# mLSTM stage of a hybrid trunk: element-wise work moved from GpSimd to VectorE, PSUM reads of h moved to ScalarE, state products moved first

## The chip, the cores and the metric

The kernel runs on one core of one Trainium2 chip. The metric is the device time of one execution in microseconds (us); less is better. The engines are named as the profile names them: PE (TensorE, matmul and transpose), PEld (TensorE's weight loads, which overlap its matmuls), DVE (VectorE), ACT (ScalarE), POOL (GpSimd) and SP (SyncE, which issues most of the transfers here).

## The reference

Two layers on a sequence of 2048 tokens with 1024 channels, in float32: first a layer with a matrix memory (mLSTM), then one with a gated linear recurrence (RG-LRU), then a final norm. The change lies in the heads of the first layer. There, for each of 4 heads:

```python
q = einsum('bshd,hde->bhse', xch, w_q) * (M_DK ** -0.5)   # xch: silu of a causal convolution of xm
k = einsum('bshd,hde->bhse', xch, w_k)
v = einsum('bshd,hde->bhse', xmh, w_v)
...
def step(carry, inp):                                     # one chunk of tokens
    C, n, m = carry
    ...
    Sm = einsum('bhtk,bhsk->bhts', qb, kb) * W
    num = decay * einsum('bhtk,bhkv->bhtv', qb, C) + einsum('bhts,bhsv->bhtv', Sm, vb)
    den = decay * einsum('bhtk,bhk->bht', qb, n) + sum(Sm)
    hb = num / max(abs(den), exp(-m_t))
    C_new = d_last * C + einsum('bhs,bhsk,bhsv->bhkv', w_last, kb, vb)
...
hh = o * h_tilde
hn = (hh - mean(hh)) * rsqrt(var(hh) + EPS) * norm_w
y = (hn + skip * xc) * silu(z)
return y @ w_out
```

A head has keys of 256 and values of 512 elements.

## The kernel before

A product of float32 operands is made as three products of a high and a low part: `split_into` rounds the source to the high part (ACT or DVE, L735 to L737) and subtracts to get the low part (DVE or POOL, L738); `mm3` (L362 to L364) issues high by high, low by high, high by low.

Three stages stand one behind another: one ahead that makes the convolved input, the gates and silu(z) and leaves them in DRAM; `phase_a2`, the stage of the heads, from about 1010 to 1724 us of the span; and from there on the output projection and the second layer. `phase_a2` goes over 4 heads, each in 8 blocks of 256 tokens, each block in 2 chunks of 128. It is software pipelined. For block i it issues, in this order:

- `loads` of block i+1: the transfers (all on SP), the splits of `xc` and `xm` into `xch`, `xcl`, `xmh`, `xml`, and a causal mask on `qb` by POOL (`affine_select`, L828). With the first block of a head come the head's four weight loads and their splits (`qwl`, `kwl` and two halves of `vwl`);
- `recur` of chunk 0 of block i: products of the masked scores with v into a PSUM tile `n`, the state products `kv` for m = 0 and 1 (one PSUM tile, so the second waits until the first was read by the DVE update of `C`), the products of q with the state's parts `Ch`, `Cl`; then DVE's denominator (`da`), `hh` and its statistics;
- `finish` of block i-1: ACT normalises `hh` (L971) with the scale and shift in `frs`, PE transposes it into PSUM (`pt`), DVE makes `y` from `pt`, the norm weight and `skx` (skip times xc), POOL multiplies by silu(z) and stores `d_y`;
- the q and k projections of block i+1 (`skx` is made by ACT ahead of them), `recur` of chunk 1 of block i (at its end come the aggregate of the statistics, `mv`, L957, and `frs`), the scores of block i+1 and its v projections (`vh`, `vl`).

The scheduler puts these into one queue for each engine, and each engine works its queue in order. The pools bound how far a block runs ahead: two buffers for `skx`, `qb`, `sz` and `y`, one for the parts of `xc` and `xm`, one PSUM tile each for `n` and `kv`.

Of the kernel before, what the change touches and what calls it, by code (L numbers as in the profile page):

```python
# [10 lines left out]
AF = mybir.ActivationFunctionType  # L11
ALU = mybir.AluOpType
# [12 lines left out]
KV = DV // P  # L25
# [263 lines left out]
class Trunk:  # L289
# [459 lines left out]
    def phase_a2(self, wq, wk, wv, D):  # L749
        tc, nc = self.tc, self.nc  # L750
        BL = 256
        NB = T // BL
        with ExitStack() as ctx:
# [21 lines left out]
            def head_weights(h):  # L775
                w = {}
                for nm, src in (("q", wq[h]), ("k", wk[h]), ("v0", wv[h, :, :, 0:256]), ("v1", wv[h, :, :, 256:512])):
                    raw = wp.tile([P, KV, 256], F32, tag="wraw", name="wraw", bufs=2)
                    nc.sync.dma_start(raw, src)
                    if nm[0] == "v":  # L780
                        j = int(nm[1])
                        if j == 0:
                            w["v"] = (wp.tile([P, KV, 512], F32R, tag="vwh", name="vwh"),
                                      wp.tile([P, KV, 512], F32R, tag="vwl", name="vwl"))
                        hi, lo = (t[:, :, j * 256:(j + 1) * 256] for t in w["v"])
                    else:
                        w[nm] = (wp.tile([P, KV, 256], F32R, tag=nm + "wh", name=nm + "wh"),
                                 wp.tile([P, KV, 256], F32R, tag=nm + "wl", name=nm + "wl"))
                        hi, lo = w[nm]
                    a = self.split_into(hi, lo, raw, "a", "v" if h == 0 and nm in ("k", "v1") else "p")  # L790
                    if h == 0 and nm in "qk":
                        self.order(a, self.tail[-4:])
                W[h] = w

            def project(h, b):
# [7 lines left out]
                def loads():  # L803
                    if h not in W:
                        head_weights(h)
                    xm = lp.tile([P, KV, BL], F32, tag="xm", name="xm")
                    xc = lp.tile([P, KV, BL], F32, tag="xc", name="xc")
                    nc.sync.dma_start(xc, D["xc"][hs, :, bs].rearrange("k p t -> p k t"))
                    nc.sync.dma_start(xm, D["xm"][hs, :, bs].rearrange("k p t -> p k t"))
                    S["qb"] = qb = lp.tile([P, 2, P], F32, tag="qb", name="qb")  # L810
                    S["db"] = db = lp.tile([P, BL], F32, tag="db", name="db")
                    nc.sync.dma_start(qb, D["q"][r0:r0 + 2].rearrange("c t -> (c t)").partition_broadcast(P)
                                      .rearrange("p (c t) -> p c t", c=2))
                    nc.sync.dma_start(db, D["dec"][r0:r0 + 2].rearrange("c t -> (c t)").partition_broadcast(P))
                    S["sz"] = sz = lp.tile([P, KV, BL], F32, tag="sz", name="sz")
                    S["o"] = o = lp.tile([P, 2, DV], F32, tag="o", name="o")
                    nc.sync.dma_start(sz, D["sz"][hs, :, bs].rearrange("k p t -> p k t"))
                    nc.sync.dma_start(o, D["o"][b * 2:b * 2 + 2, :, h * DV:(h + 1) * DV].rearrange("c p n -> p c n"))
                    for nm, x in (("xc", xc), ("xm", xm)):
                        hi = xp.tile([P, KV, BL], F32R, tag=nm + "h", name=nm + "h")  # L820
                        lo = xp.tile([P, KV, BL], F32R, tag=nm + "l", name=nm + "l")
                        fi = (h, b, nm) == (0, 0, "xc")
                        a = self.split_into(hi, lo, x, "v" if fi else "a", "v" if nm == "xc" else "p")
                        if fi:
                            self.order(a, self.tail[-4:])
                        S[nm] = (hi, lo)
                    S["xcf"] = xc
                    nc.gpsimd.affine_select(qb, qb, pattern=[[0, 2], [1, P]], compare_op=ALU.is_ge, fill=3.0e38,  # L828
                                            base=0, channel_multiplier=-1)
                    wgt = dp.tile([P, 2, P], F32, tag="wgt", name="wgt")  # L830
                    for c in range(2):
                        nc.scalar.activation(wgt[:, c], qb[:, c], AF.Exp, bias=self.gT[:, r0 + c:r0 + c + 1],
                                             scale=-1.0)
                    S["wgt"] = wgt
# [70 lines left out]
            def recur(h, b, c, S):  # L905
# [4 lines left out]
                sh, sl = (t[:, c] for t in S["sm"])  # L910
                pn = p1.tile([P, 2, 512], F32, tag="n", name="n")
                outs = tuple(pn[:, a, 0:258] for a in range(2))
                for a in range(2):
                    self.mm3(outs[a], sh, sl, vh[i][:, VA[a]], vl[i][:, VA[a]], True, ch == 0)

                def update(m):

                    kh, kl = (t[:, c] for t in S["kw"])
                    ms = slice(m * P, (m + 1) * P)
                    ps = p1.tile([P, 2, 512], F32, tag="kv", name="kv")  # L920
                    for a in range(2):
                        self.mm3(ps[:, a, 0:258], kh[:, ms], kl[:, ms], vh[i][:, VA[a]], vl[i][:, VA[a]], True, True)
                    Cm = sp.tile([P, 516], F32, tag=f"C{m}", name=f"C{m}") if ch == 0 else C[m][0]
                    C2, p2 = Cm.rearrange("p (a b) -> p a b", a=2), ps[:, :, 0:258]
                    if ch == 0:
                        nc.vector.tensor_copy(C2, p2)
                    else:
                        nc.vector.scalar_tensor_tensor(C2, C2, self.dl[:, r:r + 1], p2, op0=ALU.mult, op1=ALU.add)
                    Ch = dp.tile([P, 516], F32R, tag=f"Ch{m}", name=f"Ch{m}")
                    Cl = dp.tile([P, 516], F32R, tag=f"Cl{m}", name=f"Cl{m}")  # L930
                    self.split_into(Ch, Cl, Cm, "a", "v")
                    return Cm, (Ch, Cl)

                for m in range(2):
                    old = C.get(m) if ch > 0 else None
                    if ch < 15:
                        C[m] = update(m)
                    if ch > 0:
                        Hc, Lc = old[1]
                        qh, ql = (t[:, m, cs] for t in S["qd"])  # L940
                        for a in range(2):
                            self.mm3(outs[a], qh, ql, Hc[:, VA[a]], Lc[:, VA[a]], False, m == 1)
# [16 lines left out]
                if c == 1:  # L959
                    mv = S["mv"]  # L960
                    S["rs"] = rs = dp.tile([P, 2, 2], F32, tag="frs", name="frs")
                    nc.gpsimd.tensor_scalar(rs[:, 0], mv[:, 1], EPS, 1.0, op0=ALU.add, op1=ALU.mult)
                    nc.gpsimd.tensor_tensor(rs[:, 0], rs[:, 0], mh, op=ALU.pow)
                    nc.vector.scalar_tensor_tensor(rs[:, 1], mv[:, 0], -1.0, rs[:, 0], op0=ALU.mult, op1=ALU.mult)

            def finish(h, b, S):
                rs = S["rs"]
                y = lp.tile([P, KV, BL], F32, tag="y", name="y")
                for c in range(2):
                    hn = S["hh"][c]  # L970
                    nc.scalar.activation(hn, hn, AF.Identity, bias=rs[:, 1, c:c + 1], scale=rs[:, 0, c:c + 1])  # L971
                for j in range(2):
                    pt = pr.tile([P, 2, 2, P], F32, tag="r", name="pt")
                    for k in range(2):
                        for c in range(2):
                            ks = slice((j * 2 + k) * P, (j * 2 + k + 1) * P)
                            nc.tensor.transpose(pt[:, k, c], S["hh"][c][:, ks], self.ident)
                    for k in range(2):
                        kk = j * 2 + k
                        nc.vector.scalar_tensor_tensor(y[:, kk], pt[:, k].rearrange("p c t -> p (c t)"),  # L980
                                                       self.v("nw", h * KV + kk), S["skx"][:, kk],
                                                       op0=ALU.mult, op1=ALU.add)
                end = (h, b) == blocks[-1]
                (nc.vector if end else nc.gpsimd).tensor_tensor(y, y, S["sz"], op=ALU.mult)
                (nc.sync if end else nc.gpsimd).dma_start(D["y"][h * KV:(h + 1) * KV, :, b * BL:(b + 1) * BL].rearrange("k p t -> p k t"), y)

            blocks = [(h, b) for h in range(H) for b in range(NB)]
# [505 lines left out]
```

## Time and profile before

| | us |
|---|---|
| median of 3 runs | 3077.47 |
| lowest, highest | 3076.24, 3080.39 |
| the profiled execution | 3070.89 |
| its span, first to last instruction | 3069.1 |
| busy in the span: PE, DVE, ACT, POOL | 2935.0, 2129.9, 1460.0, 381.3 |

The profiled execution is 6.58 us below the median of the runs. Its span is the part in which instructions ran. The chain of work that ended last is on PE for 85% of the span, on DVE for 6%, on DMA for 5%, on ACT for 2%. Matmuls are pipelined and their ends are modelled, so starts are the better guide for PE.

### The profile page before, as it was taken

Reading aid. Unit: us, or ns where it says so; the run is one execution under the profiler, and the core shown is the slowest. Engines: PE = TensorE matmul, PEld = TensorE weight load, DVE = VectorE, ACT = ScalarE, POOL = GpSimd, SP = SyncE. Lnnn points to the kernel's source line nnn. Section 1 sums busy time; section 2 is a strip of 40 time slices with the busy share of each in tenths; the row PEclk is TensorE's granted clock in tenths of the full one; section 3 lists DMA queues with packets and bytes.
Section 4 is the critical chain, followed back from the end, with each engine's and each line's share of the span. In section 5 each row is a group of like instructions: output and inputs, shape, how many; then the busy total and the mean of one; then the engine's idle time right before and its main releaser. Section 6 shows DMA issues by size and latency. Waiting matters only on the chain.

```text
span 3069.1 us, 43651 instructions
## 1 busy us (share of the span) xinstructions
PE 2935.0 (96%) x15730; PEld 2511.8 (82%) x15730; DVE 2129.9 (69%) x3825; ACT 1460.0 (48%) x2386; POOL 381.3 (12%) x407
## 2 busy tenths in 40 slices
PE   6999999999999899999999899999999998899997
PEld 4799987899988898989989777877888886687786
DVE  7866789534566587777778655687779375887775
ACT  5444546323434555555555322343445233877772
POOL 0111110000000234343333100000110000110100
PEclk9999999999999999999999899999999998999999
DMA  6766677666777645354534565666666666757743
GB/s 217 254 216 232 231 249 247 201 201 208 218 227 231 185 129 164 121 166 127 159 121 124 189 189 169 188 197 214 219 216 223 213 192 215 252 184 240 239 135 127
DMA packets 308986, 600.64 MB, mean 196 GB/s; under 512 B 27808, under 2 KB 106400, under 8 KB 308768
## 3 DMA queue, kind: packets, MB, share of 16 engines
q1 hardware_dynamic: 222784, 389.79, 41.6%
q10 hardware_dynamic: 59184, 107.77, 10.0%
q0 software_dynamic: 26800, 100.28, 8.4%
q8 instruction: 124, 2.03, 0.3%
q14 instruction: 94, 0.77, 0.1%
HBM read 388.86 MB, written 208.86 MB: 195 GB/s over the span
## 4 chain that ended last, share of the span: by engine, by line
PE 85%; DVE 6%; DMA 5%; ACT 2%; issue 1%; POOL 0%; SPq 0%; ACTq 0%; DVEq 0%; POOLq 0%
PE acc L362 6%; PE acc L363 6%; PE acc L364 6%; PE pj L362 3%; PE pj L363 3%; PE pj L364 3%; PE pd L362 3%; PE pc L362 3%; PE pd L363 3%; PE pd L364 3%; PE pc L364 3%; PE pc L363 3%; PE pa L362 3%; PE pa L363 3%; PE pa L364 3%; PE pb L363 2%
## 5 line engine op out<-in xcount | busy, mean ns | idle before, releaser
L735 ACT CAST s<-raw 128x512 fp32r<-128x512 f32 (+1 forms) x360 | 222.2, 621 | 500.9 <-PE acc L364 193.4
L738 DVE TENSOR_TENSOR s<-raw,s 128x512 fp32r<-128x512 f32 (+1 forms) x360 | 246.6, 688 | 91.5 <-ACT s L735 87.2
L362 PE MATMUL acc<-yh,s 128*128 128x512 f32 x512 | 204.5, 402 | 9.9 <-DVE x L1125 3.6
L363 PE MATMUL acc<-yl,s 128*128 128x512 f32 x512 | 203.9, 398 | 0.3 <-DVE yl L738 0.3
L364 PE MATMUL acc<-yh,s 128*128 128x512 f32 x512 | 202.8, 396 | 0.0
L362 PE MATMUL acc<-yh,wh 128*128 128x512 f32 x384 | 149.7, 397 | 13.5 <-ACT yh L735 8.9
L735 ACT CAST Ch<-C 128x516 fp32r<-128x516 f32 x120 | 74.8, 623 | 171.1 <-DVE da L944 120.1
L364 PE MATMUL acc<-yh,wl 128*128 128x512 f32 x384 | 150.9, 395 | 1.1 <-DVE wl L738 1.1
L363 PE MATMUL acc<-yl,wh 128*128 128x512 f32 x384 | 151.0, 394 | 0.3 <-DVE yl L738 0.2
L662 DVE SCALAR_TENSOR_TENSOR xc<-xm,vec,xc 128x512 f32<-128x512 f32 x192 | 140.3, 746 | 14.5 <-ACT xc L660 13.4
L735 ACT CAST s<-sum 128x512 fp32r<-128x512 f32 (+1 forms) x120 | 74.3, 620 | 146.7 <-PE pa L364 43.6
L738 DVE TENSOR_TENSOR Cl<-C,Ch 128x516 fp32r<-128x516 f32 x120 | 116.7, 972 | 20.9 <-ACT Ch L735 20.7
L362 PEld LDWEIGHTS acc<-yh,s 128*128 128x128 f32 x512 | 97.8, 191 | 35.7 <-DVE x L1125 4.5
L364 PEld LDWEIGHTS acc<-yh,s 128*128 128x128 f32 x512 | 97.3, 190 | 23.2 <-DVE s L738 0.3
L363 PEld LDWEIGHTS acc<-yl,s 128*128 128x128 f32 x512 | 97.3, 190 | 22.9 <-DVE yl L738 0.8
L735 ACT CAST wh<-wr 128x512 fp32r<-128x512 f32 (+1 forms) x104 | 65.4, 641 | 102.1 <-PE acc L363 63.6
L662 DVE SCALAR_TENSOR_TENSOR xc<-xr,vec,xc 128x512 f32<-128x512 f32 x144 | 104.8, 747 | 7.3 <-ACT xc L660 6.0
L738 DVE TENSOR_TENSOR s<-sum,s 128x512 fp32r<-128x512 f32 (+1 forms) x120 | 82.4, 688 | 39.2 <-ACT s L735 38.1
L738 DVE TENSOR_TENSOR wl<-wr,wh 128x512 fp32r<-128x512 f32 (+1 forms) x104 | 73.4, 716 | 51.7 <-ACT wh L735 51.2
L362 PE MATMUL gate<-xch,wh 128*128 128x512 f32 x224 | 92.7, 415 | 16.7 <-ACT xch L735 8.8
L362 PE MATMUL pj<-vwh,xmh 128*128 128x512 f32 x256 | 103.4, 404 | 0.0
L364 PE MATMUL pj<-vwh,xml 128*128 128x512 f32 x256 | 100.5, 392 | 0.0
(419 smaller groups left out, 9684.9 us busy)
## 6 DMA issues: line engine op xcount, KB each, us to landing
d_wx<-s POOLq DMA_DIRECT2D x64, 512.0 KB, 4.1
s<-d_wx SPq DMA_DIRECT2D x64, 512.0 KB, 4.4
raw<-in_wout_dram SPq DMA_DIRECT2D x128, 256.0 KB, 3.1
raw<-in_wxz_dram SPq DMA_DIRECT2D x124, 256.0 KB, 4.5
d_wr<-s POOLq DMA_DIRECT2D x48, 512.0 KB, 3.4
s<-d_wr SPq DMA_DIRECT2D x48, 512.0 KB, 4.4
wr<-in_rwout_dram SPq DMA_DIRECT2D x96, 256.0 KB, 2.9
raw<-in_rwin_dram SPq DMA_DIRECT2D x84, 256.0 KB, 3.8
```

The source lines that it names most:

```text
L362: mm(out, sh, mh, start=first, stop=False, skip_group_check=resumed)
L363: mm(out, sh, ml, start=False, stop=False, skip_group_check=resumed)
L364: mm(out, sl, mh, start=False, stop=last, skip_group_check=resumed)
L662: nc.vector.scalar_tensor_tensor(out, x[:, j:j + TB], self.v(wn, m * 4 + j), out, op0=ALU.mult, op1=ALU.add)
L735: a = nc.scalar.copy(hi, src)
L738: b = (nc.gpsimd if lo_eng == "p" else nc.vector).tensor_tensor(lo, src, hi.bitcast(F32), op=ALU.subtract)
```

## The change

Five edits, all in `phase_a2`:

1. The low parts of all weights and of `xm` are subtracted on DVE. Before, 14 of the 16 weight pieces (each 128 x 1024) and all 32 `xml` were POOL's.
2. In `recur` the products of the scores with v (`within`) are issued behind the state products of m = 0, where they stood first before.
3. The shift in `frs` is made by two POOL instructions, a multiply by -1 and a product, where one DVE instruction made it before.
4. In `finish`, four DVE instructions for a block that made `y` out of PSUM with `skx` added become four ACT instructions that scale `pt` out of PSUM, and one DVE sum `y + skx` over 128 x 1024.
5. The product `y * sz` is DVE's in every block. Before, it was POOL's in 31 of 32.

```diff
-                    a = self.split_into(hi, lo, raw, "a", "v" if h == 0 and nm in ("k", "v1") else "p")
+                    a = self.split_into(hi, lo, raw, "a", "v")
...
-                        a = self.split_into(hi, lo, x, "v" if fi else "a", "v" if nm == "xc" else "p")
+                        a = self.split_into(hi, lo, x, "v" if fi else "a", "v")
...
-                for a in range(2):
-                    self.mm3(outs[a], sh, sl, vh[i][:, VA[a]], vl[i][:, VA[a]], True, ch == 0)
+
+                def within():
+                    for a in range(2):
+                        self.mm3(outs[a], sh, sl, vh[i][:, VA[a]], vl[i][:, VA[a]], True, ch == 0)
...
                     if ch < 15:
                         C[m] = update(m)
+                    if m == 0:
+                        within()
...
-                    nc.vector.scalar_tensor_tensor(rs[:, 1], mv[:, 0], -1.0, rs[:, 0], op0=ALU.mult, op1=ALU.mult)
+                    nc.gpsimd.tensor_scalar(rs[:, 1], mv[:, 0], -1.0, None, op0=ALU.mult)
+                    nc.gpsimd.tensor_tensor(rs[:, 1], rs[:, 1], rs[:, 0], op=ALU.mult)
...
-                        nc.vector.scalar_tensor_tensor(y[:, kk], pt[:, k].rearrange("p c t -> p (c t)"),
-                                                       self.v("nw", h * KV + kk), S["skx"][:, kk],
-                                                       op0=ALU.mult, op1=ALU.add)
+                        nc.scalar.activation(y[:, kk], pt[:, k].rearrange("p c t -> p (c t)"), AF.Copy,
+                                             scale=self.v("nw", h * KV + kk))
+                nc.vector.tensor_tensor(y, y, S["skx"], op=ALU.add)
                 end = (h, b) == blocks[-1]
-                (nc.vector if end else nc.gpsimd).tensor_tensor(y, y, S["sz"], op=ALU.mult)
+                nc.vector.tensor_tensor(y, y, S["sz"], op=ALU.mult)
```

Line numbers of the kernel after are 2 to 5 higher from L912 on.

The first place is DVE's queue in the first half of a block in the middle of a head, before:

```order
L899 TENSOR_TENSOR vl_9767<-pj,vh_9763 128x2x256
L928 SCALAR_TENSOR_TENSOR C_9991<-C_9991,dl,kv 128x516
L738 TENSOR_TENSOR Cl_10235<-C_9991,Ch_10234 128x516
L928 SCALAR_TENSOR_TENSOR C_10004<-C_10004,dl,kv 128x516
L944 TENSOR_SCALAR da<-n 128x1
L980 SCALAR_TENSOR_TENSOR y<-pt,vec,skx 128x256
L945 SCALAR_TENSOR_TENSOR da<-n,da,enT 128x1
```

And the same place in the kernel after, up to the sum with `skx`:

```order
L930 SCALAR_TENSOR_TENSOR C_9985<-C_9985,dl,kv 128x516
L899 TENSOR_TENSOR vl_9767<-pj,vh_9763 128x2x256
L738 TENSOR_TENSOR xml<-xm,xmh 128x1024
L738 TENSOR_TENSOR Cl_11322<-C_9985,Ch_11321 128x516
L930 SCALAR_TENSOR_TENSOR C_10004<-C_10004,dl,kv 128x516
L948 TENSOR_SCALAR da<-n 128x1
L949 SCALAR_TENSOR_TENSOR da<-n,da,enT 128x1
L951 RECIPROCAL da<-da 128x1
L953 SCALAR_TENSOR_TENSOR hh<-n,da,o 128x512
L738 TENSOR_TENSOR Cl_11346<-C_10004,Ch_11345 128x516
L960 BN_STATS st<-hh 128x6
L987 TENSOR_TENSOR y<-y,skx 128x1024
```

The update of `C` for m = 0 now stands ahead of `vl`, `xml` stands between `vl` and the first `Cl`, and the four `y` from PSUM, which stood between the small `da` instructions, are gone; one sum stands behind the statistics.

The second place is ACT's queue in the same half block, before:

```order
L971 ACTIVATE hh<-hh,frs 128x512 x2
L898 CAST vh_9763<-pj 128x2x256
L735 CAST xmh<-xm 128x1024
L735 CAST Ch_10234<-C_9991 128x516
L735 CAST Ch_10252<-C_10004 128x516
L850 ACTIVATE qT<-pj 128x512
L839 ACTIVATE skx<-xc,vec 128x256 x4
```

And after:

```order
L976 ACTIVATE hh<-hh,frs 128x512 x2
L735 CAST xmh<-xm 128x1024
L898 CAST vh_9763<-pj 128x2x256
L735 CAST Ch_11321<-C_9985 128x516
L985 ACTIVATE y<-pt,vec 128x256 x2
L735 CAST Ch_11345<-C_10004 128x516
L985 ACTIVATE y<-pt,vec 128x256 x2
L850 ACTIVATE qT<-pj 128x512
L839 ACTIVATE skx<-xc,vec 128x256 x4
```

`xmh` has moved ahead of `vh`, and the four `y` have come in, two on each side of the second `Ch`.

The third place is POOL's queue for one block in the kernel after; before, it held `frs` (2), the mask on `qb`, `xml`, `y<-y,sz` and the store of `d_y`:

```order
L966 TENSOR_SCALAR frs<-mv 128x2
L968 TENSOR_SCALAR frs<-mv 128x2
L967 TENSOR_TENSOR frs<-frs,mh 128x2
L969 TENSOR_TENSOR frs<-frs 128x2
L828 AFFINE_SELECT qb<-qb 128x256
L990 DMA d_y<-y 128x4x256
```

Four small instructions stand where two stood, and the two large ones are gone. In most blocks `frs` stands ahead of the mask on `qb`. Before, the mask stands ahead of `frs` twice at each of the three changes of head, in the block in which the next head's `vwl` is split and in the second block behind it; after, only the first of the two is left.

## Rows read from the trace of the kernel before

**Rows 1.** Windows: PE, PEld, DVE, ACT, POOL busy (count); clock, DMA share, GB/s.

```profile
1080.00:1170.00 90.00, 90.00 (x660) 85.16 (x660) 71.60 (x146) 52.35 (x97) 31.38 (x26) 1.00 0.42 133
```

**Rows 2.** Chain that ended last: start, us, what (one row a block).

```profile
1087.92 0.89 PE s L869 x8
...
1171.91 0.89 PE s L869 x8
...
1285.43 0.89 PE s L869 x8
...
1348.36 0.89 PE s L869 x8
...
1418.15 0.89 PE s L869 x8
```

**Rows 3.** What PE waited for, 1000 to 1760 us: in total, times, longest.

```profile
PE kv L362 <- DVE C L928: 15.5, 8, 3.2
```

**Rows 4.** Timeline of PE, middle of a block: start, us, instruction.

```profile
1107.15 0.28 PE L362 MATMUL n<-Ch,qh 128*128 128x258 f32 x1
1107.27 0.29 PE L363 MATMUL n<-Cl,qh 128*128 128x258 f32 x1
...
1107.67 0.28 PE L363 MATMUL kv<-vl,kh 128*128 128x258 f32 x1
```

**Rows 5.** Timeline of DVE, one block in mid head.

```profile
1092.16 0.17 DVE L957 BATCH_NORM_AGGREGATE mv<-st 128x2 f32<-128x6 f32 x1
...
1097.76 1.84 DVE L738 TENSOR_TENSOR Cl<-C,Ch 128x516 fp32r<-128x516 f32 x1 [0.74 <-ACT Ch L735]
1099.52 0.74 DVE L928 SCALAR_TENSOR_TENSOR C<-C,dl,kv 128x516 f32<-128x516 f32 x1
...
1102.87 0.47 DVE L980 SCALAR_TENSOR_TENSOR y<-pt,vec,skx 128x256 f32<-128x256 f32 x1
1103.27 0.68 DVE L956 BATCH_NORM_STATS2 st<-hh 128x6 f32<-128x512 f32 x1
...
1105.63 0.75 DVE L738 TENSOR_TENSOR ql<-qd,qh 128x512 fp32r<-128x512 f32 x1 [1.01 <-ACT qh L735]
1106.64 0.75 DVE L928 SCALAR_TENSOR_TENSOR C<-C,dl,kv 128x516 f32<-128x516 f32 x1 [0.26 <-PE kv L364]
```

**Rows 6.** Timeline of ACT, the same block.

```profile
1093.64 1.52 ACT L971 ACTIVATE hh<-hh,frs 128x512 f32<-128x512 f32 x2 [0.61 <-DVE frs L964]
1095.07 0.56 ACT L898 CAST vh<-pj 128x512 fp32r<-128x512 f32 x1
1095.53 1.05 ACT L735 CAST xmh<-xm 128x1024 fp32r<-128x1024 f32 x1
...
1103.38 1.71 ACT L839 ACTIVATE skx<-xc,vec 128x256 f32<-128x256 f32 x4 [0.46 <-DVE y L980]
```

**Rows 7.** Timeline of POOL, the same block.

```profile
1092.42 0.19 POOL L962 TENSOR_SCALAR frs<-mv 128x2 f32<-128x2 f32 x1 [6.43 <-DVE mv L957]
1092.69 0.71 POOL L963 TENSOR_TENSOR frs<-frs,mh 128x2 f32<-128x2 f32 x1
...
1096.66 2.38 POOL L738 TENSOR_TENSOR xml<-xm,xmh 128x1024 fp32r<-128x1024 f32 x1 [2.09 <-ACT xmh L735]
```

**Rows 8.** Timeline of DVE where the second head begins.

```profile
1171.64 3.82 DVE L738 TENSOR_TENSOR xcl<-xc,xch 128x1024 fp32r<-128x1024 f32 x1
...
1183.63 2.30 DVE L964 SCALAR_TENSOR_TENSOR frs<-mv,frs 128x2 f32<-128x2 f32 x1 [2.65 <-POOL frs L963]
...
1188.41 2.70 DVE L738 TENSOR_TENSOR Cl<-C,Ch 128x516 fp32r<-128x516 f32 x1
```

**Rows 9.** POOL, the same place: the mask, and what it waited for.

```profile
1182.11 0.41 POOL L828 TENSOR_SCALAR_AFFINE_SELECT qb<-qb 128x256 f32<-128x256 f32 x1 [7.74 <-DMA qb<-d_q]
```

**Rows 10.** Single tiles, all times: ns min/median/max, first and last start, form.

```profile
L984 DVE TENSOR_TENSOR y<-y,sz x1: 1224/1224/1224, 1722.9 to 1722.9; 128x1024 f32<-128x1024 f32 x1
L1315 POOL COPY hcarry<-xc x16: 1689/2170/3842, 2625.7 to 3014.4; 128x3 f32<-128x3 f32 x16
```

## The prediction

> **What bounds the kernel now.** I read four views, in this order. First the windows: in the middle of a head PE is busy for the whole stretch, with DVE busy for 71.60 of 90 us, ACT for 52.35 and POOL for 31.38, at full clock [rows 1]. So PE sets the pace there, and removing work elsewhere gives nothing by itself. Second the chain of waits, where the scores of each block are a mark: from 1087.92 to 1171.91 there are four blocks, 21.00 us each [rows 2]. The same marks show where time is lost. Across the first change of head, five blocks take 113.52 us where 105.00 are due [rows 2]. PE has less to do there, since the last chunk of a head makes no state products and the first has no state to read: 24 matmuls at a pitch of 0.12 us, that between the first two of [rows 4], so 2.9 us. The loss is 113.52 - 105.00 + 2.9 = 11.4 us. Across the second change three blocks take 69.79 us where 63.00 are due [rows 2], a loss of 9.7. Taking the third as the second, about 31 us are lost. Third, what PE waits for in the stage: 15.5 us in 8 waits are state products that wait for DVE's update of `C` [rows 3]. Fourth, the timelines of DVE, ACT and POOL, to see how near another loop is to PE's pace in the steady blocks.
>
> PE's own pace: of 1107.15, 1107.27 and 1107.67 the first two are one pitch, the last two are two matmuls apart and take 0.40 us where 0.24 are due [rows 4]. The wait is for the single `kv` tile, 0.16 us, and comes twice a block; without it PE would need 21.00 - 0.32 = 20.68 us.
>
> The other loop goes: aggregate of the statistics, `frs`, ACT's normalised `hh`, `vh` behind it, then DVE's chain to the last `y`, ACT's `skx` which waits for it, `qh`, `ql`, `C`, and the next aggregate. From the aggregate at 1092.16 to `skx` at 1103.38 it takes 11.22 us [rows 5, 6], and to the next aggregate 21.00 - 11.22 = 9.78, of which 0.26 is DVE's wait for PE [rows 5]. So this loop alone would run in 20.74 us. Both are within 0.3 us of the present period: a loop that grows by a few tenths takes over.
>
> **The change, in the steady blocks.** I rebuild the first part of the loop, 11.22 us, edit by edit.
>
> The shift in `frs`: a second small multiply stands ahead of the power, one pitch of 1092.42 to 1092.69, +0.27 [rows 7]. From the power's start to ACT's `hh` it took 1092.69 to 1093.64, 0.95 [rows 6, 7]. Now the power (0.71 and a little, 0.75) is followed by POOL's product of two columns and a handover of some 0.09. No row has that product; its bounds are the 0.19 of the small multiply and the 0.71 of the power [rows 7]. I take 0.25, since it is a plain product of the same size as the first. That makes 1.09, so +0.14, and with 0.71 it would be +0.60.
>
> ACT's order: between `vh` and the start of the first `Cl` lay 1095.07 to 1097.76, 2.69 us [rows 5, 6]. Now `xmh` is ahead (1.05, of which 0.1 overlaps as `vh` and `xmh` do, so 0.95 [rows 6]), then `vh` 0.56, `vl` at about the 0.68 of an instruction over as many columns [rows 5], and `xml` on DVE at 1.22 [rows 10], pitch 1.14: 3.3 us, +0.6.
>
> The first `Cl` takes 1.84 us, and its successor starts 1.76 behind it [rows 5], while POOL runs `xml` from 1096.66 to 1099.04 [rows 7]. Its neighbours over as many columns take 0.68 to 0.74. POOL's `xml` is gone, so this becomes a pitch of 0.60: -1.16.
>
> From `C` at 1099.52 to `skx` at 1103.38 it took 3.86 [rows 5, 6]. Four `y` go, at a pitch of 0.40 [rows 5], -1.60; the statistics come into the path, +0.60, and the sum over 1024 columns, +1.22 [rows 10]; and the three dependent `da` instructions lose what filled the time between them, for which I take 0.3 (between nothing and 0.6). Together +0.5. ACT's new `y` cost 0.43 each, a quarter of the 1.71 of `skx` [rows 6], and lie beside DVE's work.
>
> Sum: 0.27 + 0.14 + 0.6 - 1.16 + 0.5 = +0.35. `y * sz` on DVE (1.22) stands between `qd` and `ql`, where DVE waits 1.01 us for `qh` [rows 5]; as the wait for `skx` and `qh` remains, I cost it at nothing. The loop becomes 20.74 + 0.35 = 21.1 us. PE meanwhile loses its two waits, since 12 instead of 8 matmuls lie between the two `kv`, and would need 20.68. The loop is longer, so the period is 21.1: about +0.1 over some 24 steady blocks, **+3 us**. The bounds: if PE sets the pace, -0.32 x 24 = -8; with the product at 0.71, the loop is 21.6 and the cost +14.
>
> **At the changes of head.** Here `C` waits for `vl`, `vl` for `vh`, `vh` for `hh` on ACT, and that for `frs`, which is late because the mask ahead of it on POOL waits for its transfer [rows 9], and because DVE is held while POOL splits weights: `xcl` takes 3.82, the shift 2.30, `Cl` 2.70 [rows 8], against 1.22 for a 128 x 1024 sum [rows 10], 0.17 for an instruction over two columns and some 0.7 for `Cl` [rows 5], 6.7 us in all. With the edits `C` of m = 0 stands ahead of `vl`, so the state products no longer hang on `frs`, and one of the two late masks is behind it. The 15.5 us of PE's waits for `C` [rows 3] are what this can remove most directly. What it adds: four weight pieces on DVE, 1.22 each [rows 10], two of them with `xml` ahead of a `Cl`. For the part of these that PE sees I take 0.8 a change. **-13 us**, with 0 as the one bound (a new wait for `Cl` takes the place) and the holds as the other, 3 x 6.7 = -20.
>
> The Trainium skill says, in "SBUF — State Buffer", section "Who interferes with whom", that a DVE instruction with two SBUF inputs contends with a GpSimd instruction that reads SBUF, that the shared port is locked exclusively, and that whichever issues second blocks. By that rule the holds disappear with POOL's large instructions, as I have it, but POOL's four small ones can in their turn be blocked behind DVE's sums and subtractions, of which there are now more. The trace agrees with the first half (3.82 us for `xcl` beside POOL's split [rows 8]); the second would give the time of the first rival below.
>
> **Start and end of the stage.** At the start two weight pieces more go through DVE ahead of the first projections, 1.22 each, at least one under the wait for the loads: +1.2 at most. At the end the small products (+0.4) and the sum (+1.2) stand in the last block's path. 0 to 2.8; I take **+2**.
>
> Sum: 3 - 13 + 2 = **-8 us**. The profiled execution would be 3070.89 - 8 = 3062.9 (its span is 1.8 shorter than itself, and the profiled execution is 6.58 below the median of the runs shown). On the median: 3077.47 - 8 = **3069.5 us**.
>
> **Rivals.** *POOL's small instructions are held (slower).* `frs` is on the loop, and four instructions can now each find the port taken. For it: elsewhere in this kernel a POOL copy of 3 columns takes 1.69 to 3.84 us [rows 10], far above the 0.19 of `frs` [rows 7]. Against it: just behind the aggregate DVE works on `vl`, `kl` and `C`, which read PSUM. One hold the length of a 1.22 us sum in each block puts the period at 22.3, +1.3 x 24 = 31 in place of 3: 31 - 13 + 2 = +20, **3097.5 us**. It decides from 0.33 us a block on (8 / 24). The milder form, the product at 0.71, gives 14 - 13 + 2 = +3, 3080.5.
>
> *PE sets the pace.* If the handovers that I added overlap, the loop stays below 20.68, and the blocks gain what PE no longer waits: -8 - 13 + 2 = -19, **3058.5 us**. For it: PE is full in the window. Against it: the loop was already no shorter than PE.
>
> *The changes of head keep their length.* The weight pieces and `xml` in DVE's single queue delay `Cl`, so PE waits for the q products instead of `kv`: 3 + 0 + 2 = +5, **3082.5 us**; with half of the gain -1.5, 3076. For it: DVE has 18.4 us free in 90 [rows 1] and gets three 1.22 us instructions a block for four of 0.47, and four more at each change.
>
> **How the numbers follow.** The forecast has 0.46, PE's pace 0.18, the unchanged heads 0.20 (half of it with half the gain), the held POOL 0.16 (half of it the milder form). About 0.2%, 6.2 us, is what a measurement of this kernel can tell from no change. The forecast's own spread, some 5 us, puts two thirds of it beyond 6.2 faster: 0.31 and 0.18 from PE's pace make 0.49 faster. Slower by over 0.2% are the held form 0.08, a third of the milder and a third of the unchanged heads with all their bounds, and a little of the forecast: 0.17. The rest, 0.34, is the same. The range goes from 3056 (PE's pace with a little more at the heads) to 3083 (the heads unchanged); what is left out is the held form and the far end of the gains, under 0.2.
>
> **What would show it.** Right: the scores' period at 21.1 and PE with waits of 0.1 to 0.5 us a block for `hh` or `s`; `Cl` and `xcl` at no more than 1.3 us everywhere; no PE wait of `kv` for `C` over 1 us; `frs` on POOL from the aggregate to ACT's `hh` in about 1.6 us. Wrong: a `frs` row on POOL of a microsecond or more in the steady blocks; the period at 20.7 or above 21.4; a new wait of PE for `Cl` or `xml` at the changes of head that adds up to 10 us.

## The result and the profile after

| | before | after |
|---|---|---|
| median of 5 runs, us | 3077.47 | 3061.18 |
| lowest, highest | 3076.24, 3080.39 | 3058.01, 3063.88 |
| ratio, 95% interval | | 0.9949, 0.9937 to 0.9961 |
| the profiled execution, its span | 3070.89, 3069.1 | 3061.18, 3059.1 |

The kernel is faster by 0.51%. The forecast was 3069.5 with a range of 3056 to 3083. Between the two profiled executions, against which the sum was made, the gain is 9.7 us where 8 were forecast; between the medians it is 16.3, because the profiled execution of before lies 6.6 us below its median and that of after on it. Single runs of the kernel before lie between 3066.8 and 3085.3 us, but for one slow run of 3881.6 us at a granted clock of 0.77, which no ratio here takes in.

The scores of the 32 blocks, which were the marks in [rows 2], give the account by stretches. From the first to the last of them it took 672.6 us before and 661.2 after, so 11.4 less. A steady block takes 21.03 where it took 21.00 (medians of 21.034 and 20.995, +0.04 x 31 = +1.2); the changes of head give the rest, -12.6; start, end and what lies behind them +1.7 (-9.7 + 11.4). Forecast were +3, -13 and +2.

The loop first. The timelines of DVE, then of ACT, in the same block as [rows 5, 6], in the kernel after:

```profile
1091.45 0.17 DVE L961 BATCH_NORM_AGGREGATE mv<-st 128x2 f32<-128x6 f32 x1
...
1096.81 1.22 DVE L738 TENSOR_TENSOR xml<-xm,xmh 128x1024 fp32r<-128x1024 f32 x1
1097.94 0.69 DVE L738 TENSOR_TENSOR Cl<-C,Ch 128x516 fp32r<-128x516 f32 x1
...
1101.72 1.21 DVE L987 TENSOR_TENSOR y<-y,skx 128x1024 f32<-128x1024 f32 x1
...
1103.52 1.22 DVE L989 TENSOR_TENSOR y<-y,sz 128x1024 f32<-128x1024 f32 x1
...
1112.49 0.17 DVE L961 BATCH_NORM_AGGREGATE mv<-st 128x2 f32<-128x6 f32 x1
```

```profile
1093.23 1.52 ACT L976 ACTIVATE hh<-hh,frs 128x512 f32<-128x512 f32 x2 [0.85 <-POOL frs L969]
...
1102.97 1.71 ACT L839 ACTIVATE skx<-xc,vec 128x256 f32<-128x256 f32 x4 [0.87 <-DVE y L987]
```

From the aggregate to `skx` it takes 1102.97 - 1091.45 = 11.52 us, forecast 11.22 + 0.35 = 11.57. `Cl` is at 0.69 where it was held to 1.84. From aggregate to aggregate it is 21.04. DVE no longer waits for PE at the `C` where it waited 0.26 us [rows 5]. PE waits for that `C`, as the timelines of DVE and PE show:

```profile
1105.83 0.75 DVE L930 SCALAR_TENSOR_TENSOR C<-C,dl,kv 128x516 f32<-128x516 f32 x1
```

```profile
1106.21 0.28 PE L364 MATMUL n<-Ch,ql 128*128 128x258 f32 x1
1106.63 0.39 PE L362 MATMUL kv<-vh,kh 128*128 128x258 f32 x1
1106.85 0.28 PE L363 MATMUL kv<-vl,kh 128*128 128x258 f32 x1
```

`C` ends at 1106.58, and `kv` starts at 1106.63. Two steps of PE take 0.64 us where 0.24 are due: a wait of 0.40, where two of 0.16 stood before. So the loop has taken over from PE, at nearly the same period.

The small POOL instructions, by the view of the tile `frs` (ns min/median/max of all 32):

```profile
L966 POOL TENSOR_SCALAR frs<-mv x32: 187/188/193, 1049.6 to 1704.8; 128x2 f32<-128x2 f32 x32
L968 POOL TENSOR_SCALAR frs<-mv x32: 223/226/231, 1049.9 to 1705.0; 128x2 f32<-128x2 f32 x32
L967 POOL TENSOR_TENSOR frs<-frs,mh x32: 723/723/859, 1050.1 to 1705.2; 128x2 f32<-128x2 f32 x32
L969 POOL TENSOR_TENSOR frs<-frs x32: 195/195/197, 1050.9 to 1706.0; 128x2 f32<-128x2 f32 x32
```

None is held in the steady blocks; the longest, a power of 0.859 us, is one at the end of the stage. The product takes 0.195 us (bounds 0.19 and 0.71, taken 0.25).

At the changes of head the waits of PE for `C` are gone [rows 3], and another has come. What PE waited for, 1000 to 1760 us:

```profile
PE pt L982 <- ACT hh L976: 15.5, 5, 5.9
PE s L869 <- ACT kT L860: 7.8, 4, 5.7
...
PE kv L362 <- DVE C L930: 2.1, 6, 0.6
```

The first line holds one wait of 5.9 at the end of the stage (4.6 before) and one of about 3 at each change of head. ACT's timeline at the first of these, with the transposes of PE after it:

```profile
1181.49 0.81 ACT L976 ACTIVATE hh<-hh,frs 128x512 f32<-128x512 f32 x1 [5.07 <-POOL frs L969]
1182.21 1.03 ACT L735 CAST xmh<-xm 128x1024 fp32r<-128x1024 f32 x1
1183.15 0.58 ACT L898 CAST vh<-pj 128x512 fp32r<-128x512 f32 x1
1183.62 1.99 ACT L735 CAST vwh<-wraw 128x1024 fp32r<-128x1024 f32 x2
1185.52 0.62 ACT L735 CAST Ch<-C 128x516 fp32r<-128x516 f32 x1
1186.04 0.81 ACT L976 ACTIVATE hh<-hh,frs 128x512 f32<-128x512 f32 x1
```

```profile
1186.91 1.54 PE L982 MATMUL pt<-ident,hh 128*128 128x128 f32 x6 [3.29 <-ACT hh L976]
```

ACT stands idle for 5.07 us before the first half of the normalised `hh`, since `frs` is late, and only then turns to `xmh`, `vh` and the weights, which wait for nothing of it; the second half of `hh` stands behind them, and PE waits 3.29 us for that.

### The profile page after: what moved, and what is told of

Its sections match the earlier page's. It is cut to its first block, busy times and chain, and to the rows that moved or that the text cites. A ratio compares the mean times of both kernels' runs of the same rounds, so it can differ in the third digit from the quotient of the medians.

```text
span 3059.1 us, 43718 instructions
## 1 busy us (share of the span) xinstructions
PE 2927.9 (96%) x15730; PEld 2506.7 (82%) x15730; DVE 2153.6 (70%) x3774; ACT 1509.3 (49%) x2514; POOL 211.7 (7%) x394
## 5 line engine op out<-in xcount | busy, mean ns | idle before, releaser
L930 DVE SCALAR_TENSOR_TENSOR C<-C,dl,kv 128x516 f32<-128x516 f32 x112 | 83.7, 747 | 44.6 <-PE kv L364 44.5
```

## The experiments

The theory after the result, ahead of these runs: the split of the gain is as the account has it, and two statements explain it. (A) The holds of DVE by POOL and the order of the state products both cost time at the changes of head. (L) In the steady blocks the loop through `frs`, `hh`, `y + skx` and `skx` sets the period, a little above the 20.7 that PE would need. Rivals are in the expectations. In the table the period is the median step between the marks; the loss at the changes of head is the way from first to last mark less 31 periods, plus 3 x 2.9 us for the work that PE lacks there. Ratios are to runs of the kernel before on the same chip. Those runs had medians of 3074.7 to 3077.5 us, so times of different rows compare to some 3 us.

| edits | median, us | ratio (95%) | period | first to last mark | loss at heads |
|---|---|---|---|---|---|
| none (before) | 3077.47 | 1 | 21.00 | 672.6 | 30 |
| all (after) | 3061.18 | 0.9949 (0.9937 to 0.9961) | 21.03 | 661.2 | 18 |
| 1, weights alone | 3059.34 | 0.9958 (0.9943 to 0.9973) | 21.01 | 661.7 | 19 |
| 1 | 3050.17 | 0.9905 (0.9881 to 0.9929) | 21.00 | 651.6 | 9 |
| 2 | 3075.16 | 0.9994 (0.9980 to 1.0007) | 21.31 | 676.7 | 25 |
| 1, 2 | 3043.90 | 0.9885 (0.9863 to 0.9906) | 20.66 | 639.7 | 8 |
| 1, 2, 3 | 3057.68 | 0.9950 (0.9934 to 0.9967) | 20.68 | 656.3 | 24 |
| 1, 2, 5 | 3055.52 | 0.9944 (0.9929 to 0.9958) | 21.09 | 649.6 | 4.5 |
| 1, 3, 4, 5 | 3081.92 | 1.0018 (1.0006 to 1.0030) | 21.74 | 680.1 | 15 |
| 1, 2, 4, 5 | 3043.61 | 0.9895 (0.9868 to 0.9921) | 20.68 | 641.8 | 9 |
| 1, 2, 3, 5 | 3059.51 | 0.9949 (0.9931 to 0.9966) | 20.68 | 658.5 | 26 |
| 1, 2, 3, 4 | 3069.06 | 0.9982 (0.9969 to 0.9996) | 21.02 | 668.2 | 25 |
| all, third `skx` buffer | 3060.60 | 0.9958 (0.9944 to 0.9973) | 21.03 | 657.1 | 14 |
| all, two more on `frs` | 3077.14 | 1.0011 (0.9998 to 1.0024) | 21.61 | 676.6 | 15 |

**Second edit undone.** In the kernel after:

```diff
+                within()
...
-                    if m == 0:
-                        within()
```

> The kernel after with the second edit undone: the products of the scores with v stand first again. Theory A (both the holds that POOL's large instructions caused and the place of the state products cost time at the changes of head): state products wait for C again, 1 to 2 us once or twice at each change of head, so the scores' marks across the three changes grow by 4 to 6 us in all; in the steady blocks there are two short kv waits instead of one, but the loop through frs and skx sets the period, so it stays at 21.0 to 21.1. Time 5 us above the kernel after. Theory B (the holds alone cost the time): no kv wait over 1 us, the marks as in the kernel after, within 2 us of it. Theory C (the order alone gave the gain): 11 us above it.

It is 20 us above the kernel after, far more than each theory had, and in the steady blocks, not at the changes of head. The timelines of DVE and PE in this kernel:

```profile
1097.36 1.23 DVE L738 TENSOR_TENSOR xml<-xm,xmh 128x1024 fp32r<-128x1024 f32 x1 [2.65 <-ACT xmh L735]
1098.50 0.69 DVE L899 TENSOR_TENSOR vl<-pj,vh 128x512 fp32r<-128x512 f32 x1
1099.10 0.74 DVE L932 SCALAR_TENSOR_TENSOR C<-C,dl,kv 128x516 f32<-128x516 f32 x1
```

```profile
1099.90 0.39 PE L362 MATMUL kv<-vh,kh 128*128 128x258 f32 x1 [0.66 <-DVE C L932]
```

`xml` and `vl` now stand ahead of `C`, in a queue worked in order, and the second `kv` waits 0.64 to 0.67 us in the steady blocks: the period is 21.74. What the second edit buys beside the others is that `C` does not hang on `xmh` and `vh`.

**First edit alone.** The kernel before with

```diff
-                    a = self.split_into(hi, lo, raw, "a", "v" if h == 0 and nm in ("k", "v1") else "p")
+                    a = self.split_into(hi, lo, raw, "a", "v")
...
-                        a = self.split_into(hi, lo, x, "v" if fi else "a", "v" if nm == "xc" else "p")
+                        a = self.split_into(hi, lo, x, "v" if fi else "a", "v")
```

> The kernel before with the first edit alone: all low parts on VectorE. Theory A: no instruction of VectorE is held over 1.3 us by the splits; the product with silu(z) is still on GpSimd and can hold one; the three changes of head lose 5 to 8 us each in place of 10; about 6 us faster than the kernel before. Theory B: 11 us faster, with changes of head like those of the kernel after. Theory C: no faster; the four splits on VectorE cost what the holds cost.

27 us faster than before, more than any theory had and more than the whole change. The loss at the changes of head falls from 30 to 9 us, about the 3 x 6.7 of the holds, which the prediction had set as the far bound. What PE still waited for:

```profile
PE pt L977 <- ACT hh L971: 8.4, 4, 4.6
PE s L869 <- ACT kT L860: 4.4, 1, 4.4
PE kv L362 <- DVE C L928: 3.6, 3, 1.9
```

The 15.5 us of waits for `C` are 3.6 with the order of before: they came from the holds and the late mask, and the order was not needed to remove them. A second mask that stood ahead of `frs` is behind it in this kernel too, so holds and mask are not told apart by this run; two runs below do that in part.

**Second edit alone.** The kernel before with the second edit of the diff.

> The kernel before with the second edit alone: state products of m = 0 first. Theory A: the waits of PE for C at the changes of head (15.5 us in 8 waits) fall to under 4 us, but the holds of xcl, frs and Cl stay (6.7 us a change) and turn into waits for hh and Cl; 5 us faster than the kernel before, of it nothing to 4 us in the steady blocks, where PE loses one or both of its two waits of 0.16 us. Theory B: no faster. Theory C: 11 us or more faster.

No measurable difference (0.9980 to 1.0007). The holds stay in sum, but all of them now lie on `Cl`, which the expectation did not have: `xcl` takes 1.23 us at most and the shift 0.16, while three `Cl` at the first change of head take 3.27, 2.45 and 2.90. The first of them, beside POOL's split of `kwl` (1173.10 to 1175.50):

```profile
1172.79 3.27 DVE L738 TENSOR_TENSOR Cl<-C,Ch 128x516 fp32r<-128x516 f32 x1
```

With `kv` first the waits move to other places:

```profile
PE s L869 <- ACT kT L860: 15.2, 4, 7.8
PE kv L362 <- DVE C L929: 12.8, 24, 1.0
PE pt L980 <- ACT hh L974: 4.6, 1, 4.6
PE kv L362 <- ACT vh L898: 3.8, 3, 1.3
```

The 7.8 of the first line are at the start of the stage, where 7.5 stood before. The period even grows, to 21.31. In this kernel no mask on `qb` stands ahead of `frs` at a change of head, and the loss there is still 25: without a late mask, the holds are enough for it. Theory A had 5 us for this edit; theory C falls.

**First and second edit.**

> The kernel before with the first two edits; frs, the y out of PSUM and the product with silu(z) as they were. Theory A: nearly all of the gain, 9 to 13 us faster than the kernel before, the changes of head as in the kernel after within 1 us each. Rival (the y edits carry the gain, because GpSimd's product with silu(z) still holds VectorE's two-input instructions): no more than half, 6 us, with xcl or Cl at 2 us or more in every block.

33 us faster than before, where theory A had 13 at most, and 17 faster than the whole change. The aggregates, a block apart, on DVE's timeline:

```profile
1086.91 0.17 DVE L960 BATCH_NORM_AGGREGATE mv<-st 128x2 f32<-128x6 f32 x1
...
1107.59 0.17 DVE L960 BATCH_NORM_AGGREGATE mv<-st 128x2 f32<-128x6 f32 x1
```

20.68 us: PE's own pace as the prediction worked it out from [rows 4]. So what the second edit gives beside the first lies in the steady blocks (21.00 to 20.66), and only 1 us of it at the changes of head. Edits three to five take back about half of what the first two give, both in the steady blocks (0.37 x 31 = 11 us) and at the changes of head (10 us). The next runs look for the one that does it.

**Third edit undone**, in the kernel after:

```diff
-                    nc.gpsimd.tensor_scalar(rs[:, 1], mv[:, 0], -1.0, None, op0=ALU.mult)
-                    nc.gpsimd.tensor_tensor(rs[:, 1], rs[:, 1], rs[:, 0], op=ALU.mult)
+                    nc.vector.scalar_tensor_tensor(rs[:, 1], mv[:, 0], -1.0, rs[:, 0], op0=ALU.mult, op1=ALU.mult)
```

> The kernel after with the third edit undone: the shift in frs is one VectorE instruction again. Theory L (the loop from the aggregate through frs, hh, VectorE's sum with skx and ACT's skx sets the period of 21.03 in the kernel after, while PE alone would need 20.66 as with the first two edits alone): the way from the aggregate to hh falls from 1.78 to about 1.48 us, the loop to 20.73 and the period with it; 24 blocks by 0.30 are 7 us, and about 1 us at each change of head: 7 to 10 us faster than the kernel after. Rival P (PE sets the period, and the sums and products on VectorE have changed PE's own pace or order): the period stays at 21.03, no faster. Rival Q (the queue of VectorE is simply full: the work moved there is too much): slower by the 0.16 us added, or unchanged.

18 us below the kernel after, so all of what was lost. The loop is what theory L made it, 20.75 by the aggregates, here of two blocks in the third head:

```profile
1422.28 0.17 DVE L961 BATCH_NORM_AGGREGATE mv<-st 128x2 f32<-128x6 f32 x1
...
1443.03 0.18 DVE L961 BATCH_NORM_AGGREGATE mv<-st 128x2 f32<-128x6 f32 x1
```

The median between the marks is lower, 20.68, because PE is ahead of the loop after a change of head and goes at its own pace until the loop holds it (20.70 and 20.74 in the last two blocks). The changes of head gain 8 us, which no theory had. ACT's timeline at the first of them shows what is different:

```profile
1176.54 1.05 ACT L735 CAST xmh<-xm 128x1024 fp32r<-128x1024 f32 x1 [1.95 <-PE pj L363]
1177.49 0.58 ACT L898 CAST vh<-pj 128x512 fp32r<-128x512 f32 x1
1177.97 1.99 ACT L735 CAST vwh<-wraw 128x1024 fp32r<-128x1024 f32 x2
1180.10 0.63 ACT L735 CAST Ch<-C 128x516 fp32r<-128x516 f32 x1
1180.63 1.52 ACT L975 ACTIVATE hh<-hh,frs 128x512 f32<-128x512 f32 x2
```

The scheduler has put both halves of `hh` behind `xmh`, `vh` and the weights. ACT does these while `frs` is late and waits for nothing at `hh`; in the kernel after it idled 5.07 us ahead of them. The mask stands ahead of `frs` in both. The other kernels agree: in all seven with the third edit, ACT idles 3.35 to 6.28 us for `frs` at each change of head; in the five that have the first edit, or its first half, without the third, it idles 1.97 us there at most.

**Fourth edit undone**, in the kernel after:

```diff
-                        nc.scalar.activation(y[:, kk], pt[:, k].rearrange("p c t -> p (c t)"), AF.Copy,
-                                             scale=self.v("nw", h * KV + kk))
-                nc.vector.tensor_tensor(y, y, S["skx"], op=ALU.add)
+                        nc.vector.scalar_tensor_tensor(y[:, kk], pt[:, k].rearrange("p c t -> p (c t)"),
+                                                       self.v("nw", h * KV + kk), S["skx"][:, kk],
+                                                       op0=ALU.mult, op1=ALU.add)
```

> The kernel after with the fourth edit undone: y is made out of PSUM by four VectorE instructions with skx added, as before. Theory L: skx waits for the last of these instead of the statistics and the sum; the loop loses 0.6 us and falls to 20.4, below PE's 20.66, which sets the period: 0.37 by 28 blocks are 10 us, and some us at the changes of head; 10 to 16 us faster than the kernel after. Rival P: period 21.03, no faster. Rival Q: VectorE's work grows by 4 x 0.40 less 1.14 a block, 0.5 us, so the period grows by as much: 12 us slower.

The period falls to PE's, as theory L had it, and rival Q falls with it: DVE does more, and the blocks are shorter. But the changes of head lose 26 us, 8 more than in the kernel after, and the time is the same. PE waited 15.8 us for `hh` in 8 waits, 4.9 of them at the end of the stage. In this kernel the mask is again ahead of `frs` twice at a change, as before, and one of POOL's small instructions is held at each change, as under the first three edits below.

**Fifth edit undone**: the product with silu(z) on POOL again, in the kernel after.

> The kernel after with the fifth edit undone: the product with silu(z) is GpSimd's again in 31 of 32 blocks. Theory L: it is not on the loop, and GpSimd's 2.4 us lie beside VectorE's wait for qh; the period stays at 21.03 to 21.15, the time within 3 us of the kernel after. Rival Q (VectorE's queue is full): 1.14 us less VectorE work a block shortens the period to PE's 20.66, 10 us faster. Rival H (holds by the shared port): ql or xcl is held by 1 us or more in each block, and the period grows to 22: 25 us slower.

The period stays at 21.02, so it is not on the loop, and DVE's queue is not what is full. Rival H falls too: `ql` is held at the changes of head alone, once each, at 1.53 us. The changes of head lose 25 us in place of 18, and the time lies 8 us above the kernel after. So this edit is worth something beside the third and fourth.

**Third buffer for `skx`**, `bufs=3` on the tile in the kernel after.

> The kernel after with a third buffer for skx, so that ACT's skx of the next block no longer waits for VectorE's sum with the skx of the block before last. Nothing else is changed, though the scheduler interleaves skx differently. Theory L: the loop is cut at this place, and what is left of it is shorter than PE's pace: period 20.66 to 20.75, 8 to 14 us faster than the kernel after. Rival P: period 21.03. Rival Q: unchanged, since VectorE has the same work.

The period is 21.03, but the run does not decide between the theories: ACT still starts `skx` at the end of DVE's sum (1100.37 + 1.21 = 1101.58), so the loop was not cut. Why the wait stays with three buffers is open.

```profile
1101.61 0.91 ACT L839 ACTIVATE skx<-xc,vec 128x256 f32<-128x256 f32 x2 [1.40 <-DVE y L987]
```

**Two more small instructions on `frs`**, the other way to test the loop: lengthen it. In the kernel after:

```diff
                     nc.gpsimd.tensor_tensor(rs[:, 1], rs[:, 1], rs[:, 0], op=ALU.mult)
+                    nc.gpsimd.tensor_scalar(rs[:, 1], rs[:, 1], 1.0, None, op0=ALU.mult)
+                    nc.gpsimd.tensor_scalar(rs[:, 1], rs[:, 1], 1.0, None, op0=ALU.mult)
```

> The kernel after with two more small GpSimd instructions on the way of frs: the shift is multiplied by 1 twice. Theory L (the loop through frs sets the period of 21.03): each costs a pitch of 0.25 to 0.28 us, as between the first two instructions of frs, so the period becomes 21.5 to 21.6 and the time grows by 12 to 16 us. Rival P (PE's own pace is 21.03): a delay of half a microsecond on GpSimd is hidden; period 21.03, no slower.

```profile
1089.98 0.18 DVE L961 BATCH_NORM_AGGREGATE mv<-st 128x2 f32<-128x6 f32 x1
...
1111.60 0.17 DVE L961 BATCH_NORM_AGGREGATE mv<-st 128x2 f32<-128x6 f32 x1
```

The period is 21.61 (21.62 between these two), longer by 0.58 for two instructions of 0.21, and the time is 16 us above the kernel after. Theory L holds, rival P falls.

**First three edits.**

> The first three edits alone: low parts on VectorE, state products first, the shift in frs on GpSimd; y out of PSUM on VectorE and the product with silu(z) on GpSimd as before. Theory L: in the steady blocks the loop of the first two edits alone (about 20.1 us by its rows, PE at 20.66) takes the 0.30 us of the shift without becoming the longer one, so the period stays at 20.66 to 20.7; at the changes of head, where frs is late, the 0.3 us shows and, if the shift on GpSimd is what makes PE wait there for the normalised hh (2.8 to 3.3 us in the kernel after, at most 0.6 with the first two edits alone), 2 us or more each. So 1 to 8 us slower than the first two edits alone. Rival (the third edit costs its 0.30 us in each block whatever stands beside it): period 20.97, 10 us or more slower than the first two edits alone.

The period stays at PE's 20.68: with `y` made on DVE the loop has room for the shift, so edits three and four cost the 0.37 us a block only together. The rival falls. The changes of head lose 24 us in place of 8, more than expected: 14 us in the time. Half of `hh` again stands ahead of the weights on ACT, which idles 4.64 us for `frs` ahead of it. A second thing shows in the block behind, on DVE and on POOL:

```profile
1196.54 1.22 DVE L738 TENSOR_TENSOR xcl<-xc,xch 128x1024 fp32r<-128x1024 f32 x1
```

```profile
1196.62 1.22 POOL L968 TENSOR_SCALAR frs<-mv 128x2 f32<-128x2 f32 x1
```

POOL's multiply over two columns takes 1.22 us in place of 0.23: it starts 0.08 us behind DVE's `xcl` and ends 0.08 behind it. This happens at each of the three changes of head, here and with the fourth edit undone, and PE then waits 1.1 to 1.2 us for `vh` and `vl`.

**Edits one, two and five.**

> Edits one, two and five: the third and fourth undone. Theory L: neither the shift nor the sum with skx is on the loop any more, and the product with silu(z) on VectorE lies in the wait for qh: period 20.66 to 20.7. At the changes of head: if the fifth edit is what costs there, 3 to 6 us in all against the first two edits alone; if not, the same within 2 us. Rival Q (VectorE's queue is full): the period grows by up to the 1.14 us of the product.

Here theory L was wrong: the period is 21.09. The scheduler has put `vl` ahead of `C` again, and `kv` waits for it:

```profile
1095.75 0.69 DVE L899 TENSOR_TENSOR vl<-pj,vh 128x512 fp32r<-128x512 f32 x1 [1.67 <-ACT vh L898]
1096.36 0.74 DVE L930 SCALAR_TENSOR_TENSOR C<-C,dl,kv 128x516 f32<-128x516 f32 x1
```

The changes of head lose 4.5 us, the least of all. Yet the mask stands ahead of `frs` twice at each of them, as in the kernel before; POOL's timeline has the second:

```profile
1220.08 0.40 POOL L828 TENSOR_SCALAR_AFFINE_SELECT qb<-qb 128x256 f32<-128x256 f32 x1 [8.87 <-DMA qb<-d_q]
1220.57 0.19 POOL L966 TENSOR_SCALAR frs<-mv 128x2 f32<-128x2 f32 x1
```

So in this kernel, with the first two edits in place, the late masks cost little. This run also took 378.9 us for the output projection behind the stage, where the kernel after took 372.1.

**Weights alone**: the first half of the first edit, in the kernel before.

> The kernel before with the low parts of the weights alone on VectorE; xml stays on GpSimd. Theory W (the gain of the first edit at the changes of head is that GpSimd's weight splits no longer hold xcl, the shift and Cl): the holds of 3.82 and 2.30 us are gone, most of the gain of the first edit is there, 15 to 22 of its 27 us, with the steady period at 21.00. Rival X (xml matters as much, since it stands ahead of the mask or holds Cl in every block): no more than 10 us of the 27.

16 us faster than before, of the 27 of the whole first edit; in the time theory W holds. Of the two holds that it named only that of `xcl` is gone. The shift, on DVE, is still held: it starts beside POOL's `xml` and ends with it.

```profile
1178.05 2.29 DVE L964 SCALAR_TENSOR_TENSOR frs<-mv,frs 128x2 f32<-128x2 f32 x1 [3.22 <-POOL frs L963]
```

```profile
1177.99 2.33 POOL L738 TENSOR_TENSOR xml<-xm,xmh 128x1024 fp32r<-128x1024 f32 x1
```

With `xml` still on POOL, the waits for `C` stay (14.1 us in 9), and the loss at the changes is 19 us in place of 9. The mask is ahead of `frs` once at a change here, as with the whole first edit, so these 10 us are `xml`'s and not the mask's; in the 11 us from the kernel before to this one, weights and second mask go together.

## Why the prediction was right, and where its parts were not

**The loop in the steady blocks: right, and shown.** The rebuilt way of 11.57 us was 11.52, and the rest of the loop 9.52, as worked out. The largest error of its parts is that from the aggregate to `hh`, 1.78 in place of 1.89, with the product at 0.195 in place of 0.25. The term was +3 and is +1.2. That the loop sets the period is shown by three runs: two more instructions lengthen it by what they take, without the third edit it is 20.75 by the aggregates, and without the fourth the period falls to PE's pace. Where PE meets the loop was not foreseen: the prediction looked for waits at `hh` or `s`, and PE waits 0.40 us for `C`.

**PE's pace: right.** 20.68 was read from the waits at `kv`, and the kernels in which nothing else is longer run at 20.66 to 20.68.

**The changes of head: the size right, the reason not.** The term was -13 and is -12.6, but as the sum of two larger ones, so that the number is luck. The prediction gave the gain to the order of the state products, with the 15.5 us of waits as the measure, and took the holds as a bound. The runs show it the other way: the first edit alone takes 21 us off the loss, the second alone 5, which it loses again in the steady blocks, and beside the first only 1. One hold it put down wrongly: the 2.30 us of the shift [rows 8] come from POOL's `xml`, not from the weights, since they stay when the weights alone are moved. Then edits three to five give about 10 back, a term that the prediction did not have. The third does this: the kernels with the first two edits lose 14 to 26 us with it and 4.5 to 9 without it. That it does so by the order of ACT's queue at a late `frs` is what the timelines with and without it show; that exactly this order costs it was not tried by itself.

**Start and end: the number by luck**, +2 and +1.7. The first mark comes 0.1 us earlier, and from the last mark to the output projection it takes 0.5 longer. The rest of the 1.7 is the output projection, 3.6 shorter, and what follows it, 4.9 longer, which no edit touches.

**The rivals.** POOL's small instructions are not held in the steady blocks; the most in the stage is 859 ns, for one power. The Trainium skill's rule on the shared port ("SBUF — State Buffer", section "Who interferes with whom") agrees on the side that helped: without POOL's large instructions no `Cl` is above 0.70 us and no `vwl` above 1.36. On the other side the Trainium skill says in the same section that a VectorE instruction with at most one SBUF input, outside the 2-port modes, does not contend with GpSimd. The trace agrees: those around `frs` in the steady blocks have one input in PSUM, and none of the `frs` is held. Where `xcl`, with both inputs in SBUF, fell beside `frs`, in two runs at each change of head, POOL's multiply was held to 1.22 us. So the mechanism of this rival exists, and in the kernel after such a pair hardly ever meets. PE's pace was the right rival for two edits of the five, and its period did not come true for all, though the measured 3061.2 lies nearer to its 3058.5 than to the forecast's 3069.5. The unchanged heads did not come true.

**The medians.** The gain between the medians is 16.3 us, twice the 8 of the forecast, and the sum answers for 9.7 of it. The 6.6 us by which the gain between the medians exceeds that between the profiled executions is no work of the change that a trace shows. The profiled execution of before is within the 18 us over which single runs of that kernel spread.

## What to carry to other kernels

When a change has several edits, a term can come out right as the sum of two that were not foreseen, here -22 and +10 us at the changes of head; run the edits alone, since here two of the five gave 33 us and all of them 16. A small instruction on the longest loop costs its whole time in each round even where its engine stands idle for most of the time, and where PE is barely the bound a tenth of a microsecond decides who sets the pace. When a scheduler fixes each engine's order, look after each edit at what it put behind the one instruction that is known to be late: where a 0.16 us instruction moved to another engine, the order of ACT's queue changed and the changes of head took 8 us more.

## What was not expected of the hardware

The output projection behind the stage, which no kernel here changes, took from 370.0 to 378.9 us between its first and last matmul, with a mean granted clock of 1.00 in the shortest and 0.98 in the longest: differences of several us between single executions of these kernels say nothing of an edit. A GpSimd instruction over two columns cost a pitch of 0.29 us on the loop (0.58 for two), though it runs for 0.21. One such instruction that started 0.08 us behind a VectorE subtract over 128 x 1024 took 1.22 us, as long as the subtract.
